# RWKV-7 recurrence in a hybrid block: state-free chunk products in one batch, and three VectorE instructions placed behind the product emitted last

## The chip, the cores and the metric

One NeuronCore of a Trainium2 chip runs the whole program in one launch. The metric is the device time in microseconds (us), lower is better.

## What is computed

A hybrid transformer block on 1024 tokens of width 1024: a forgetting attention and an RWKV-7 time mix side by side, then a gated convolutional feed-forward network. The change lies in the time mix, whose core is a recurrence over the tokens with a 64 x 64 state per head, 8 heads:

```python
def step(state, inp):
    r_t, w_t, k_t, v_t, a_t, b_t = inp
    sa = jnp.einsum('bhvk,bhk->bhv', state, a_t)
    state = state * w_t[:, :, None, :] + sa[..., None] * b_t[:, :, None, :] + v_t[..., None] * k_t[:, :, None, :]
    y_t = jnp.einsum('bhvk,bhk->bhv', state, r_t)
    return state, y_t
```

Here `w` is the decay, `a` the negated normalised key, `b` the normalised key times a learned rate. The result `y` is normalised per head, scaled, and gated. All values are float32.

## The kernel before

**Stages.** An opening stage normalises and modulates the input into `u`. Then come small low-rank products, then the recurrence, then the attention, the branch and output products, and the feed-forward network. Long products (128 x 512, float32r, each operand as a high and a low part, three products per pair) make up most of TensorE's work: the recurrence stage also holds the projections `ps_rkv`, `qk` and `gt` and the 256-wide `v`, all of them products with `u`, whose only task beside their own is to fill TensorE while a step of the recurrence waits.

**The recurrence.** Two heads and 512 tokens (half of the sequence, `hf`) make a unit; 4 head pairs `p` and 2 halves give 8 units, numbered `k` from 0. A unit is 8 chunks of 64 tokens. `pre` (L725) does what needs no state: it loads the log decays and rates (`cum`, `al`, L738 and L740), sums the decays by a scan on VectorE (L741) and exponentiates them on ScalarE, normalises the keys by `head_sums` (product `ssq`), multiplies keys by queries and rates chunk by chunk (product `p` into `E`, L786), and inverts the triangular 64 x 64 matrix of each chunk. The inversion takes 32 x 32 diagonal blocks: they go through DRAM scratch to a layout with one block per partition (`sm`, `M32`, L797 to L801), a substitution of 31 steps on VectorE, two instructions each (L809 writes `t`, L811 updates `E32`), and through DRAM again into `TT` (`se`, L814 and L822). Then follow transposes (`vt`, `at`, `tb`), the product `q` and the sums `bs`.

`main` (L855) joins the blocks: two VectorE transposes of `TT` into `X` (L866), the products `xi` and `zi`, then `uw`, then `mz`, which gives the two matrices `Zt` and `Mt` that take a state through a chunk. After that comes a loop over the 8 chunks. Each chunk has two kinds of small products into the PSUM tiles `sp` (next state) and `yp` (output): state-free ones (`sp<-UV,E`, `yp<-E,UV`, in `fixed`, L912) and ones with the state `S0` (`sp<-S,Mt`, `yp<-Zt,S`, L925 and L932). VectorE scales `sp` into the next state `S` (L929), which the next chunk's products need. `mu` and `va` close a unit by its normalisation.

**What sets the order.** TensorE runs in the order of emission. The class `Weave` (L48) emits: it keeps a nominal clock `now` in nanoseconds, adds a nominal cost for each product (`mm_cost`), and runs generators ("chains"). A chain emits a step and yields how long it wants to wait; until the next chain is due, `fill` emits long products. The main chain has rank 1 and the pre chain rank 2; a spawned chain has rank 0. VectorE, ScalarE, GpSimd and SyncE (which issues the transfers) get their order in this stage from the framework's scheduler: each instruction is placed by simulated times, after the ones that it depends on, and each engine then runs its own list strictly in that order.

The unit's `ready` (L802) is the nominal time before which `xi` is not emitted: 46000 ns (unit 0) or 38500 ns after the transfers into `M32`.

Of the kernel before, what the change touches and what calls it, by code (L numbers as in the profile page):

```python
# [9 lines left out]
F32 = mybir.dt.float32  # L10
# [37 lines left out]
class Weave:  # L48
# [67 lines left out]
    def run(self, chains):  # L116

        self.live = [[self.now, 1 + i, g] for i, g in enumerate(chains)]
        while self.live:
            due = min((c for c in self.live if c[0] <= self.now), key=lambda c: (c[1], c[0]), default=None)  # L120
            if due is None:
                self.fill(min(c[0] for c in self.live))
                continue
            wait = next(due[2], None)
            if wait is None:
                self.live.remove(due)
            else:
                due[0] = self.now + max(wait, 0.0)
# [3 lines left out]
def hybrid_block(ctx: ExitStack, tc: tile.TileContext, a, out):  # L132
# [4 lines left out]
    def mm(o, lhsT, rhs, start, stop, more=False):  # L137

        weave.mm_cost(o, lhsT, rhs)
        nc.tensor.matmul(o, lhsT, rhs, start=start, stop=stop, skip_group_check=more)  # L140
# [194 lines left out]
    with ExitStack() as es:  # L335
# [388 lines left out]

        def pre(k, p, hf):  # L725
# [15 lines left out]
            nc.vector.tensor_tensor_scan(cum, C("reset"), cum, initial=0.0, op0=ALU.mult, op1=ALU.add)  # L741
            el = chunk_tile("el", 1, NCU, CH + 1)
            nc.gpsimd.memset(el[:, :, 0:1], 1.0)
            nc.scalar.activation(el[:, :, 1:], c3(cum), AF.Exp, scale=-DEC)
            en = tmp("en")
            nc.scalar.activation(en, cum, AF.Exp, scale=DEC)
# [5 lines left out]
            yield from head_sums(ssq, ksq, parts[:, 0, :], parts[:, 1, :])  # L752
            rn = tmp("ksq")
# [48 lines left out]
            ready = weave.now + (46000 if k == 0 else 38500)  # L802
            E32 = chunk_tile("E32", 1, 8, 32)
            nc.gpsimd.tensor_copy(E32, C("einit").rearrange("p (j t) -> p j t", t=32))
            t32 = tmp("t32", 256)
            for s in range(31):
                J, W = s // 4 + 1, 31 - s
                tv = t32[:, 0 : J * W].rearrange("p (j w) -> p j w", w=W)
                tt(tv, E32[:, 0:J, s : s + 1].to_broadcast([128, J, W]),  # L809
                   M32[:, s : s + 1, s + 1 : 32].to_broadcast([128, J, W]), op=ALU.mult)  # L810
                tt(E32[:, 0:J, s + 1 : 32], E32[:, 0:J, s + 1 : 32], tv, op=ALU.add)  # L811
            se = scr.tile([2, NCU, 2, 32, 32], F32, tag="se", name=f"se{n}")
            for g in range(4):
                nc.sync.dma_start(  # L814
                    se.rearrange("h c b (j g) t -> (h c b) g j t", g=4)[:, g, :, :],
                    E32[g * 32 : g * 32 + 32, :, :])
            TT = chunk_tile("TT", 2, NCU, CH)
            for h in range(2):
                nc.gpsimd.memset(TT[h * 64 + 32 : h * 64 + 64, :, 0:32], 0.0)
                for b in range(2):  # L820
                    r0 = h * 64 + b * 32
                    nc.sync.dma_start(TT[r0 : r0 + 32, :, b * 32 : b * 32 + 32],  # L822
                                      se[h, :, b, :, :].rearrange("c s t -> s c t"))

# [30 lines left out]
        def main(k, p, hf):  # L855
# [8 lines left out]
            B1 = (slice(32, 64), slice(96, 128))  # L864
            for h in range(2):
                nc.vector.transpose(X[B0[h], :, :], TT[B0[h], :, 0:32])  # L866
            yield max(0, o["ready"] - weave.now)
# [44 lines left out]
            def fixed(c):  # L912

                alone = hf == 0 and c == 0
                for h in range(2):
                    mm(sp[HS[h], c, :], E[:, c, h, 2, :], UV[:, c, h, :], start=True, stop=alone)
# [1078 lines left out]
```

## Time and profile before

| what | us |
|---|---|
| median of 3 runs (lowest, highest) | 1701.3 (1697.85, 1704.96) |
| profiled execution, its own time | 1704.73 |
| its span in the trace | 1703.0 |
| TensorE busy, weight loads, VectorE, ScalarE, GpSimd | 1638.0, 1342.0, 1220.8, 808.6, 143.4 |
| recurrence stage in the trace | 151 to 655 |

How to read it: PE is TensorE, PEld its weight loads, DVE VectorE, ACT ScalarE, POOL GpSimd, SP the engine that issues most transfers. A row names the line, the engine, the operation, what it writes and reads (`sp<-UV,E`), the shape, the count, the busy time or the duration, and the idle time ahead of it with what ended it. Matmuls are pipelined and their ends are modelled, so the step from one start to the next tells the rate, not the duration. The small float32 products stand as two rows each, and those of the two heads start together.

### The profile page before, as it was taken

The numbers are of one execution on the slowest core, as the hardware profiler recorded it, in microseconds if no ns is written. First come the engines' busy times: TensorE is split into PE (matmuls) and PEld (weight loads), VectorE is DVE, ScalarE is ACT, GpSimd is POOL, SyncE is SP. The second block draws the span as 40 slices with busy tenths as digits, with TensorE's granted clock in tenths as the row PEclk, the third lists the DMA queues.
The fourth block names the chain that finished last, engine by engine and source line by source line (L and its number), as shares of the span: only waits on it lengthen the run. The fifth ranks groups of instructions, "written<-read, shape, count | busy, mean of one in ns | idle before, by whom it ended". The sixth has DMA issues, their size and how long they took to land.

```text
span 1703.0 us, 26042 instructions
## 1 busy us (share of the span) xinstructions
PE 1638.0 (96%) x9772; PEld 1342.0 (79%) x9772; DVE 1220.8 (72%) x2390; ACT 808.6 (47%) x1482; POOL 143.4 (8%) x175
## 2 busy tenths in 40 slices
PE   5899999998999998999999999999999999999998
PEld 4767777786877776988878888888888888888886
DVE  5776787778676633888877634897777777787677
ACT  5453334333444554766642323654444444454455
POOL 0010101110111003123112000000000000000000
PEclk8899999999999999999999999999999999999999
DMA  8487743533342326433277611132333233484463
GB/s 328 139 314 205 192 125 97 136 106 106 91 115 75 91 81 151 141 110 107 76 265 268 246 62 63 50 105 94 123 107 103 93 117 101 163 284 153 125 215 112
DMA packets 120974, 239.85 MB, mean 141 GB/s; under 512 B 39888, under 2 KB 48336, under 8 KB 120848
## 3 DMA queue, kind: packets, MB, share of 16 engines
q1 hardware_dynamic: 112896, 220.94, 40.0%
q0 software_dynamic: 7952, 17.25, 3.8%
q8 instruction: 77, 1.26, 0.3%
q14 instruction: 49, 0.40, 0.1%
HBM read 172.59 MB, written 65.54 MB: 140 GB/s over the span
## 4 chain that ended last, share of the span: by engine, by line
PE 79%; DVE 9%; DMA 6%; ACT 2%; issue 2%; SPq 1%; DVEq 0%; ACTq 0%
PE X L140 13%; PE D L140 12%; PE Y L140 6%; PE wo L140 5%; PE br L140 5%; PE gt L140 5%; PE rk_ps L140 4%; PE qk L140 4%; PE ps_rkv L140 4%; PE W L140 3%; PE lg L140 2%; PE v L140 2%; PE ov L140 2%; PE sp L140 2%; PE tp L144 2%
## 5 line engine op out<-in xcount | busy, mean ns | idle before, releaser
L140 PE MATMUL D<-op,op 128*128 128x512 f32 x924 | 209.8, 390 | 0.0
L140 PEld LDWEIGHTS D<-op,op 128*128 128x128 f32 x924 | 173.5, 188 | 36.2 <-DVE op L1258 0.3
L140 PE MATMUL X<-T_m,S 128*128 128x512 f32 x440 | 107.3, 390 | 0.2
L140 PEld LDWEIGHTS X<-T_m,S 128*128 128x128 f32 x440 | 82.5, 188 | 18.2 <-ACT x L1534 0.6
L1257 ACT CAST op<-g 128x512 fp32r<-128x512 f32 x77 | 47.8, 621 | 74.1 <-PE D L140 48.0
L1258 DVE TENSOR_TENSOR op<-g,op 128x512 fp32r<-128x512 f32 x77 | 53.0, 689 | 41.7 <-ACT op L1257 41.7
L1494 DVE SCALAR_TENSOR_TENSOR c<-ab,vec,c 128x512 f32<-128x512 f32 x88 | 65.9, 750 | 19.5 <-ACT c L1497 17.9
L809 DVE TENSOR_TENSOR t<-E,M 128x60 f32<-128x60 f32 (+24 forms) x248 | 57.9, 233 | 30.2 <-DMA M<-sm 24.9
L1458 DVE TENSOR_TENSOR S<-ur,S 128x512 fp32r<-128x512 f32 x66 | 45.5, 691 | 35.6 <-ACT S L1454 35.5
L263 DVE TENSOR_TENSOR lo_in<-raw_in,hi_in 128x512 fp32r<-128x512 f32 x84 | 56.5, 707 | 16.1 <-PE gt L140 13.9
L1454 ACT CAST S<-ur 128x512 fp32r<-128x512 f32 x66 | 41.0, 622 | 55.6 <-DVE ur L1447 30.6
L1458 DVE TENSOR_TENSOR A<-ur,A 128x512 fp32r<-128x512 f32 x64 | 44.1, 688 | 30.9 <-ACT A L1454 30.7
L261 ACT CAST hi_in<-raw_in 128x1024 fp32r<-128x1024 f32 x42 | 44.0, 1049 | 44.3 <-PE ps_rkv L140 16.0
L140 PE MATMUL Y<-T_h,A 128*128 128x512 f32 x264 | 63.5, 390 | 0.0
L140 PE MATMUL Y<-T_h,S 128*128 128x512 f32 x264 | 63.3, 390 | 0.0
L140 PE MATMUL X<-B_b,A 128*128 128x512 f32 x252 | 60.8, 391 | 0.0
L140 PE MATMUL W<-B_f,A 128*128 128x512 f32 x252 | 60.6, 390 | 0.0
L1079 ACT ACTIVATE P<-lg,nm 128x896 f32<-128x896 f32 (+3 forms) x64 | 47.4, 743 | 22.8 <-DVE nm L1075 22.6
L811 DVE TENSOR_TENSOR E<-E,t 128x60 f32<-128x60 f32 (+24 forms) x248 | 53.8, 217 | 5.8
L140 PEld LDWEIGHTS Y<-T_h,A 128*128 128x128 f32 x264 | 49.6, 188 | 10.3
L140 PEld LDWEIGHTS Y<-T_h,S 128*128 128x128 f32 x264 | 49.6, 188 | 10.3
L1454 ACT CAST A<-ur 128x512 fp32r<-128x512 f32 x64 | 39.9, 623 | 34.2 <-PE X L140 31.5
(473 smaller groups left out, 4169.0 us busy)
## 6 DMA issues: line engine op xcount, KB each, us to landing
raw_in<-in_w_in SPq DMA_DIRECT2D x50, 512.0 KB, 3.7
wm<-in_w_mod SPq DMA_DIRECT2D x48, 512.0 KB, 7.0
ur<-in_w_up SPq DMA_DIRECT2D x44, 512.0 KB, 4.2
g<-d_g SPq DMA_DIRECT2D x35, 512.0 KB, 4.0
d_g<-gs SPq DMA_DIRECT2D x44, 256.0 KB, 2.0
d_g<-c SPq DMA_DIRECT2D x33, 256.0 KB, 4.4
d_st<-qh SPq DMA_DIRECT2D x64, 128.0 KB, 2.5
d_gate<-gs SPq DMA_DIRECT2D x32, 256.0 KB, 2.9
```

The source lines that it names most:

```text
L140: nc.tensor.matmul(o, lhsT, rhs, start=start, stop=stop, skip_group_check=more)
L144: nc.tensor.transpose(o, i, eye)
L261: nc.scalar.copy(hi, raw)
L263: nc.vector.tensor_tensor(lo[:, c : c + NH], raw[:, c : c + NH], f32(hi[:, c : c + NH]), op=ALU.subtract)
L809: tt(tv, E32[:, 0:J, s : s + 1].to_broadcast([128, J, W]), M32[:, s : s + 1, s + 1 : 32].to_broadcast([128, J, W]), op=ALU.mult)
L811: tt(E32[:, 0:J, s + 1 : 32], E32[:, 0:J, s + 1 : 32], tv, op=ALU.add)
L1079: nc.scalar.activation(e[:, 0:n], lg[:, 0:n], AF.Exp, bias=nm[:, 0:1], accum_out=nm[:, 1:2])
L1257: nc.scalar.copy(hi, src)
L1258: tt(lo, src, f32(hi), op=ALU.subtract)
L1454: nc.scalar.copy(hi, src)
L1458: tt(lo, src, f32(hi), op=ALU.subtract)
L1494: stt(c, ab[:, x + hf * NH : x + hf * NH + NH], V("conv_w", 22 * x + i), c, op0=ALU.mult, op1=ALU.add)
```

## The change

Four edits, all in the recurrence:

- **State-free products in one go.** `fixed` is gone. All 8 chunks' state-free products stand directly behind `mz`; the loop over the chunks holds only the products with the state. Only the first chunk's products open the accumulation of the two PSUM banks.
- **VectorE instructions behind the product emitted last.** A helper `behind` adds an ordering without a semaphore between a VectorE instruction and the last emitted matmul, so that the scheduler does not place it earlier. It is used for the scan of the decays (now also emitted after `ssq` instead of ahead of it), the first instruction of the substitution, and the two transposes into `X` (now emitted 1500 nominal ns ahead of `xi`, before at the head of `main`).
- **The inversion as a chain of its own**, `inverse`, spawned 8500 nominal ns after the transfers into `M32`; `ready` of unit 0 goes from 46000 to 47500.
- **`beside`.** A due step of the pre chain is held back, with fill, if a step of the main chain or of a spawned chain comes within 2600 nominal ns, and follows that step without fill between.

```diff
-    def run(self, chains):
+    def run(self, chains, beside=0.0):
...
+        led = False
         while self.live:
             due = min((c for c in self.live if c[0] <= self.now), key=lambda c: (c[1], c[0]), default=None)
-            if due is None:
-                self.fill(min(c[0] for c in self.live))
+            lead = min((c[0] for c in self.live if c[1] < 2), default=None)
+            if due is None or (due[1] > 1 and not led and lead is not None and lead < self.now + beside):
+                self.fill(min(c[0] for c in self.live) if due is None else lead)
+                led = False
                 continue
+            led = beside > 0 and (led or due[1] < 2)
...
-        nc.tensor.matmul(o, lhsT, rhs, start=start, stop=stop, skip_group_check=more)
+        weave.last = nc.tensor.matmul(o, lhsT, rhs, start=start, stop=stop, skip_group_check=more)
+
+    def behind(i):
+        tc.add_manual_dep(i.ins, weave.last.ins.name, NOSYNC)
...
+        def inverse(n, M32, TT, chunk_tile, tmp):
...
+                i = tt(tv, E32[:, 0:J, s : s + 1].to_broadcast([128, J, W]),
+                   M32[:, s : s + 1, s + 1 : 32].to_broadcast([128, J, W]), op=ALU.mult)
+                if s == 0:
+                    behind(i)
+                tt(E32[:, 0:J, s + 1 : 32], E32[:, 0:J, s + 1 : 32], tv, op=ALU.add)
...
-            nc.vector.tensor_tensor_scan(cum, C("reset"), cum, initial=0.0, op0=ALU.mult, op1=ALU.add)
-            el = chunk_tile("el", 1, NCU, CH + 1)
...
             yield from head_sums(ssq, ksq, parts[:, 0, :], parts[:, 1, :])
+            behind(nc.vector.tensor_tensor_scan(cum, C("reset"), cum, initial=0.0, op0=ALU.mult, op1=ALU.add))
+            el = chunk_tile("el", 1, NCU, CH + 1)
...
-            ready = weave.now + (46000 if k == 0 else 38500)
+            ready = weave.now + (47500 if k == 0 else 38500)
             TT = chunk_tile("TT", 2, NCU, CH)
+            weave.spawn(inverse(n, M32, TT, chunk_tile, tmp), 8500)
...
+            yield max(0, o["ready"] - weave.now - 1500)
             for h in range(2):
-                nc.vector.transpose(X[B0[h], :, :], TT[B0[h], :, 0:32])
-            yield max(0, o["ready"] - weave.now)
+                behind(nc.vector.transpose(X[B0[h], :, :], TT[B0[h], :, 0:32]))
+            yield 1500
...
-            def fixed(c):
-
+            for c in range(NCU):
                 alone = hf == 0 and c == 0
                 for h in range(2):
-                    mm(sp[HS[h], c, :], E[:, c, h, 2, :], UV[:, c, h, :], start=True, stop=alone)
+                    mm(sp[HS[h], c, :], E[:, c, h, 2, :], UV[:, c, h, :], start=c == 0, stop=alone, more=True)
                 for h in range(2):
-                    mm(yp[HS[h], c, :], UV[:, c, h, :], E[:, c, h, 1, :], start=True, stop=alone)
-
-            fixed(0)
+                    mm(yp[HS[h], c, :], UV[:, c, h, :], E[:, c, h, 1, :], start=c == 0, stop=alone, more=True)
...
-                    fixed(c + 1)
...
-        weave.run([main_chain(), pre_chain()])
+        weave.run([main_chain(), pre_chain()], beside=2600.0)
```

Lines below the first edits move down (the product helper from L140 to L144, the transposes into `X` from L866 to L881). The counts of products, transfers and VectorE instructions stay the same, and so do TensorE's order ahead of unit 0's `xi` and all order behind the last unit. Stretches of long products between small ones in the recurrence go from 133 to 123.

**TensorE, unit 1 behind `mz`.** Before, each chunk's state-free products (`sp<-UV,E`, `yp<-E,UV`) stand between long products (`qk`) and that chunk's products with the state (`S`):

```order
L140 MATMUL mz_14_2840<-E_1_1785,Wt_1_2764 64x128 x8
L140 MATMUL sp_1_2852<-UV_1_1787,E_1_1785 64x64 x2
L140 MATMUL yp_1_2851<-E_1_1785,UV_1_1787 64x64 x2
L140 MATMUL qk_0_2824<-u_hi,hi_in_2480 128x512 x6
L140 MATMUL qk_0_2824<-u_lo,hi_in_2480 128x512 x6
L140 MATMUL sp_1_2852<-S_07_2419,Mt_1_2828 64x64 x2
L140 MATMUL yp_1_2851<-Zt_1_2827,S_07_2419 64x64 x2
L140 MATMUL qk_0_2824<-u_lo,hi_in_2480 128x512 x2
L140 MATMUL qk_0_2824<-u_hi,lo_in_2481 128x512 x4
L140 MATMUL sp_1_2852<-UV_1_1787,E_1_1785 64x64 x2
L140 MATMUL yp_1_2851<-E_1_1785,UV_1_1787 64x64 x2
L140 MATMUL sp_1_2852<-S_10_2884,Mt_1_2828 64x64 x2
```

Now, at the same place (the first two small rows stand eight times in a row):

```order
L144 MATMUL mz_14_2843<-E_1_1783,Wt_1_2788 64x128 x8
L144 MATMUL sp_1_2855<-UV_1_1785,E_1_1783 64x64 x2
L144 MATMUL yp_1_2854<-E_1_1783,UV_1_1785 64x64 x2
...
L144 MATMUL ssq_1_2813<-kp_1_2761,blk_r 128x512 x2
L144 MATMUL qk_0_2782<-u_hi,lo_in_2464 128x512 x5
L144 MATMUL qk_1_2930<-u_hi,hi_in_2463 128x512 x5
L144 MATMUL sp_1_2855<-S_07_2427,Mt_1_2831 64x64 x2
L144 MATMUL yp_1_2854<-Zt_1_2830,S_07_2427 64x64 x2
L144 MATMUL qk_1_2930<-u_hi,hi_in_2463 128x512 x3
L144 MATMUL qk_1_2930<-u_lo,hi_in_2463 128x512 x3
L144 MATMUL sp_1_2855<-S_10_2938,Mt_1_2831 64x64 x2
L144 MATMUL yp_1_2854<-Zt_1_2830,S_10_2938 64x64 x2
```

The state-free products have left the loop; six long products still separate one state step from the next, and the pre chain's `ssq` now follows small products directly.

**VectorE, the transposes into `X` of unit 4.** Before, they stand in the middle of unit 3's state steps (`S`) and of the next keys (`kr`, `ar`, `bk`):

```order
L762 SCALAR_TENSOR_TENSOR ar_1_4250<-kr_1_4247,nkk,el_1_4162 128x512
L352 MEMSET sh_rkv_4451 128x1
L929 TENSOR_SCALAR S_11_4305<-sp_1_4237,pcd_1_2866 128x64
L763 SCALAR_TENSOR_TENSOR kr_1_4247<-kr_1_4247,vec,al_1_4159 128x512
L866 STREAM_TRANSPOSE X_0_4698<-TT_0_3868 32x256
L764 TENSOR_TENSOR bk_1_4249<-kr_1_4247,en_1_4165 128x8x64
L767 TENSOR_SCALAR al_1_4159<-al_1_4159,vec,oka 128x512
...
L929 TENSOR_SCALAR S_12_4321<-sp_1_4237,pcd_1_2866 128x64
```

Now they stand behind unit 3's last state step, behind the masks of the products `p` (L823) and the copies of the transposes `at` (L850):

```order
L941 TENSOR_SCALAR S_16_4410<-sp_1_4231,pcd_1_2911 128x64
...
L959 SCALAR_TENSOR_TENSOR y_1_4424<-mu_1_4426,y_1_4424 128x512
L823 TENSOR_TENSOR E_1_4427<-p_2_104_4491,cst_120 128x4x128
L823 TENSOR_TENSOR E_1_4427<-p_2_114_4492,cst_120 128x4x128
L992 TENSOR_TENSOR vs_0_4505<-v_0_4463,vs_0_4505 128x4x64
L850 COPY QA_1_4428<-at_1_4546 64x4x64 x4
L881 STREAM_TRANSPOSE X_0_4601<-TT_0_3837 32x256 x2
L992 TENSOR_TENSOR vs_1_4568<-v_1_4509,vs_1_4568 128x4x64
L968 SCALAR_TENSOR_TENSOR y_1_4424<-y_1_4424,vec,rs_1_4591 128x512
```

The first transpose stood two rows behind the state step `S_11` of unit 3, and the second three rows on; now both stand together, behind five more state steps.

**VectorE, the scan of unit 5.** Before, it stands early in unit 4's substitution (`t`, `E`), ahead of weight parts (`lo_in`) and of an evacuation (`k<-ps_rkv`):

```order
L852 TENSOR_TENSOR bon_0_4049<-bs_0_3960,v_2739 128x512
L811 TENSOR_TENSOR E_0_3798<-E_0_3798,t_0_3800 128x2x25
L809 TENSOR_TENSOR t_0_3800<-E_0_3798,M_0_3793 128x48
L741 SCALAR_TENSOR_TENSOR cum_1_4157<-cst_120,cum_1_4157 128x512
L811 TENSOR_TENSOR E_0_3798<-E_0_3798,t_0_3800 128x2x24
L263 TENSOR_TENSOR lo_in_4078<-raw_in_4075,hi_in_4077 128x512 x2
L809 TENSOR_TENSOR t_0_3800<-E_0_3798,M_0_3793 128x69
L358 SCALAR_TENSOR_TENSOR k_3355<-ps_rkv_4020,omu,sh_rkv_4071 128x512
```

Now it stands near the end of that substitution, behind the evacuations of `mz` (L919, L920):

```order
L919 TENSOR_TENSOR Zt_1_4206<-mz_14_4219,ar_1_2902 128x256
L920 TENSOR_TENSOR Mt_1_4207<-mz_14_4219,cst_120 128x256
...
L740 TENSOR_TENSOR t_0_3967<-E_0_3965,M_0_3832 128x28
L781 SCALAR_TENSOR_TENSOR cum_1_4157<-cst_120,cum_1_4157 128x512
L744 TENSOR_TENSOR E_0_3965<-E_0_3965,t_0_3967 128x7x4
...
L800 TENSOR_TENSOR ar_1_4278<-r_3376,el_1_4267 128x512
```

The scan moved from the 8th to the 28th of the substitution's 31 steps, and the `ar` that needs its exponentials (`el`) follows four rows behind it.

More of the change, by code (lines that the diff above doesn't have):

```diff
@@ L924, in main @@
                     for h in range(2):
-                        mm(sp[HS[h], c, :], Mt[HS[h], c, :], S0[HS[h], :], start=False, stop=True)
+                        mm(sp[HS[h], c, :], Mt[HS[h], c, :], S0[HS[h], :], start=False, stop=True, more=True)
                 S1 = None
@@ L931, in main @@
                     for h in range(2):
[L932 removed]
+                        mm(yp[HS[h], c, :], S0[HS[h], :], Zt[HS[h], c, :], start=False, stop=True, more=True)
                 if c + 1 < NCU:
                     yield 1150
[L935 removed]
                 S0 = state[p] = S1
```

48 lines of the change are left out of this document (23 added, 25 removed).

## The prediction

> **What bounds the kernel now.** I read the page first, then the waits of TensorE (PE) and VectorE (DVE) in the recurrence stage, then the busy time by stretches, and last the timeline at single places. The page:
>
> ```profile
> PE 1638.0 (96%) x9772; PEld 1342.0 (79%) x9772; DVE 1220.8 (72%) x2390; ACT 808.6 (47%) x1482; POOL 143.4 (8%) x175
> ```
>
> PE is the bound, and all work behind the last unit keeps its order, so the change can win only what PE loses in the stage from 151 to 655 us. Busy time there and in three short stretches (length; PE, PEld, DVE, ACT, POOL; granted clock, DMA share, GB/s):
>
> ```profile
> 151.00:655.00 504.00, 486.29 (x4349) 387.77 (x4348) 338.16 (x964) 214.19 (x374) 57.17 (x78) 0.99 0.41 113
> 228.00:238.00 10.00, 7.02 (x78) 5.16 (x78) 6.74 (x22) 2.96 (x7) 0.72 (x3) 0.83 0.48 133
> 417.00:430.00 13.00, 9.54 (x72) 6.82 (x70) 7.46 (x18) 2.86 (x4) 1.97 (x4) 0.87 0.27 75
> 528.00:538.00 10.00, 7.65 (x57) 5.20 (x56) 5.91 (x13) 3.11 (x5) 0.40 (x1) 0.83 0.27 72
> ```
>
> PE stands still for 504.0 - 486.3 = 17.7 us, and around three of the waits its granted clock drops. Who PE waited for in the stage (total, times, longest), and below it DVE's waits for transfers:
>
> ```profile
> PE sp L140 <- DVE S L929: 8.6, 5, 3.5
> PE xi L140 <- DVE X L866: 3.0, 2, 1.6
> PE p L140 <- DVE bk L769: 2.0, 1, 2.0
> PE ps_rkv L140 <- DVE k L358: 1.6, 1, 1.6
> PE at L144 <- DVE E L789: 1.0, 1, 1.0
> PE qk L140 <- DVE ql L384: 0.9, 1, 0.9
> ```
>
> ```profile
> DVE t L809 <- DMA M<-sm: 24.9, 7, 6.7
> DVE X L866 <- DMA TT<-se: 23.3, 12, 4.9
> DVE cum L741 <- DMA cum<-d_lora: 10.8, 5, 5.5
> ```
>
> Every wait of PE is for DVE, and DVE itself stood 59 us (24.9 + 23.3 + 10.8) at the head of its list waiting for transfers. These are the three instructions that the change moves.
>
> **The state-free products.** One chunk's turn before (start, length), its weight loads, and two groups of the stage (count, busy, mean ns, idle ahead): the state-free products and `q`, the nearest batch of like shape.
>
> ```profile
> 255.02 0.34 PE L140 MATMUL sp<-UV,E 128*64 128x64 f32 x4
> 255.19 0.29 PE L140 MATMUL yp<-E,UV 128*64 128x64 f32 x4
> 255.40 0.33 PE L140 MATMUL sp<-S,Mt 64*64 64x64 f32 x4
> 255.57 0.28 PE L140 MATMUL yp<-Zt,S 64*64 64x64 f32 x4
> 255.78 0.73 PE L140 MATMUL ps_rkv<-u_hi,hi_in 128*128 128x512 f32 x2
> 257.37 0.34 PE L140 MATMUL sp<-UV,E 128*64 128x64 f32 x4
> ```
>
> ```profile
> 255.02 0.20 PEld L140 LDWEIGHTS sp<-UV,E 128*64 128x64 f32 x4 [0.44 <-DVE S L929]
> ...
> 255.13 0.20 PEld L140 LDWEIGHTS yp<-E,UV 128*64 128x64 f32 x4
> ```
>
> ```profile
> L140 PE MATMUL sp<-UV,E 128*64 128x64 f32 x256 | 21.6, 248 | 8.6 <-DVE S L929 8.6
> ...
> L140 PE MATMUL q<-UV,E 64*64 64x64 f32 x256 | 10.0, 222 | 0.1
> ```
>
> From the first state-free product to the first one with the state pass 255.40 - 255.02 = 0.38 us. In a batch the next chunk's loads follow at the pace of these loads, 0.11 us for each four rows, so a chunk takes 0.22 to 0.23 us and nothing is paid for going over to the 64-row form. At `q`'s rate a chunk's 8 of 256 rows take 8 x 10.0 / 256 = 0.31 us. The saving is 0.07 to 0.16 us a chunk; I take 0.15, since the loads are of the very same products. The first chunk of each of the 8 units stands behind `mz` as before, so 7 x 8 = 56 chunks count: 56 x 0.15 = **8.4 us** (3.9 to 9.0). What covered the state's round trip through DVE stays: the first state-free product of a chunk waited for `S` as well (the row has all 8.6 us of those waits), behind the same six long products.
>
> The Trainium skill, page "TensorE: Matmul & The Clock Gate", section "Part 3: Packing small matmuls — row/col tiling", speaks against the batch: a weight load overlaps running products only when it goes to other rows of the array, and these products use all 128. By that rule this term would be about zero. The trace disagrees: loads of 0.20 us and products of 0.34 and 0.29 us for two such groups fit into 0.38 us, so they overlap already.
>
> **Fewer changes between long and small products.** A long product's own pace, from the largest group of the page:
>
> ```profile
> L140 PE MATMUL D<-op,op 128*128 128x512 f32 x924 | 209.8, 390 | 0.0
> ```
>
> 209.8 / 924 = 0.227 us. The six between 255.78 and 257.37 took 1.59 us where 6 x 0.227 = 1.36, so going in and out costs 0.23. The new order has 10 stretches of long products fewer (133 to 123). Small products that meet directly still pay something, as the step from the state-free to the state form does (0.38 - 0.23 = 0.15 at most). I take 0.14 each, **1.4 us** (0.8 to 2.3).
>
> **DVE's waits for transfers.** How one of them reaches PE, on DVE and then on PE:
>
> ```profile
> 417.18 0.74 DVE L763 SCALAR_TENSOR_TENSOR kr<-kr,vec,al 128x512 f32<-128x512 f32 x1
> 421.72 0.43 DVE L866 STREAM_TRANSPOSE X<-TT 32x256 f32<-32x256 f32 x1 [3.80 <-DMA TT<-se]
> ...
> 423.68 0.28 DVE L929 TENSOR_SCALAR S<-sp,pcd 128x64 f32<-128x64 f32 x1
> ```
>
> ```profile
> 424.02 0.47 PE L140 MATMUL sp<-UV,E 128*64 128x64 f32 x4 [3.46 <-DVE S L929]
> ...
> 425.25 2.44 PE L140 MATMUL ps_rkv<-u_hi,lo_in 128*128 128x512 f32 x5
> 427.53 0.40 PE L140 MATMUL ps_rkv<-u_hi,hi_in 128*128 128x512 f32 x1
> ```
>
> The same instructions at three more places, with DVE's wait in brackets:
>
> ```profile
> 393.11 1.23 DVE L741 TENSOR_TENSOR_SCAN cum<-cst,cum 128x512 f32<-128x512 f32 x1 [2.98 <-DMA cum<-d_lora]
> ```
>
> ```profile
> 488.37 0.43 DVE L866 STREAM_TRANSPOSE X<-TT 32x256 f32<-32x256 f32 x1 [4.16 <-DMA TT<-se]
> ```
>
> ```profile
> 531.54 0.43 DVE L866 STREAM_TRANSPOSE X<-TT 32x256 f32<-32x256 f32 x1 [3.17 <-DMA TT<-se]
> ```
>
> At 421.72 a transpose whose `X` no product needs before this chunk loop is over holds the state step behind it, and PE stands 3.46 us. Of the five waits for `S` one more is of this kind, behind 531.54: 2.35 us in the stretch 528 to 538 (10.00 - 7.65). The scan at 393.11 does the same to `k` (1.6), the transpose at 488.37 to `E` (1.0), and unit 0's transposes are late themselves (3.0). Together 3.46 + 2.35 + 1.6 + 1.0 + 3.0 = **11.4 us**. Behind the change the transposes stand behind the state steps and the scan follows its transfer by about 4.7 nominal us, so the first four waits go; of unit 0's, where PE comes eight long products (8 x 0.227 = 1.8 us) later, I leave 1.0. That is 10.4 us. What was hidden under these waits is short: DVE's own arrears at the other three `S` waits (8.6 - 5.8 = 2.8 us), which I leave as they are, as I do `p` and `qk`.
>
> **The clock.** From 424.02 to 427.53 pass 3.51 us, where a chunk's turn (255.78 - 255.02 = 0.76) and five long products (5 x 0.227) take 1.90: 1.6 us lost to the lower clock. The three stretches above with 0.83 to 0.87 lie behind three waits that go; 3 x 1.6 = **4.8 us** (0 to 4.8). The Trainium skill, page "TensorE: Matmul & The Clock Gate", section "What's actually happening", puts the throttle behind an idle window of about 3.4 us; by that only the 3.46 us wait would count and the term would be 1.6. The rows show it behind 2.35 us too, so the measurement decides.
>
> **What the change adds.** The substitution starts 8500 nominal ns behind the transfers into `M32`, and the transposes come only 1.5 us ahead of `xi`. For unit 5, whose margin is among the smallest:
>
> ```profile
> L801 SPq DMA_DIRECT2D M<-sm x4: 364/416/425, 444.5 to 445.8; - x4
> ```
>
> ```profile
> 448.90 1.16 DVE L809 TENSOR_TENSOR t<-E,M 128x31 f32<-128x31 f32 x1 [3.00 <-DMA M<-sm]
> ```
>
> ```profile
> L140 PE MATMUL xi<-X,E x32: 190/191/213, 497.2 to 497.7; 32*32 32x32 f32 x32
> L866 DVE STREAM_TRANSPOSE X<-TT x2: 433/434/436, 488.4 to 489.4; 32x256 f32<-32x256 f32 x2
> ```
>
> `X` is done at 489.8 and `xi` starts at 497.2, a margin of 7.4 us. The first substitution step moves from 448.9 to 444.5 + 8.5 = 453.0, 4.1 us later; the unit's chunk loop, shorter by 7 x 0.15, and the 1.0 us wait before it take some 2 more. About 1 us is left, less if DVE, which carries the same 338 us in a shorter stage, is slower with the chain, more since the 3.0 us that it lost at 448.9 now do other work. Some units will wait; the scan, moved behind `ssq`, also delays `p`:
>
> ```profile
> L741 DVE TENSOR_TENSOR_SCAN cum<-cst,cum x8: 1211/1224/1226, 155.8 to 507.3; 128x512 f32<-128x512 f32 x8
> L744 ACT ACTIVATE el<-cum x8: 630/632/634, 157.1 to 508.6; 128x512 f32<-128x512 f32 x8
> ```
>
> 1.22 and 0.63 us go onto that way. From unit 2 on `p` waits for the last state step of the unit two before (L777) anyway; in units 0 and 1 PE's wait at `p` can grow by these 1.9 us. SP's transfers behind a late `se` carry weights that are needed 48 products (11 us) later. I book **4 us** of new waits (0 to 12).
>
> **Sum.** 8.4 + 1.4 + 10.4 + 4.8 - 4.0 = 21 us. The profiled execution took 1704.7 us (span 1703.0), so 1683.7 by its own time; it lies 3.4 us above the median of 1701.3, so I forecast **1681 us**, with 1671 (9.0 + 2.3 + 11.4 + 4.8 and the arrears of 2.8 = 30.3, no new waits) to 1687 (the batch at 7, a third of the clock term gone, 8 us of new waits: 7 + 1.4 + 10.4 + 3.2 - 8 = 14.0) as this case's own range.
>
> **Rivals.** (1) *The waits come back elsewhere.* DVE works as much in a stage that is 4% shorter, and three of five waits for `S` already had no transfer ahead of them. If all 11.4 us of waits and their clock return at other places, the products alone win 8.4 + 1.4 = 9.8: about 1691 (1685 to 1697). That the three orderings name the wrong instructions falls under it; the rows of the waits speak against it. (2) *`xi` waits in every unit.* The substitution of unit 5 takes from 448.9 to the transposes at 488.4 with transfers, 40 us. If, denser with the state steps, it stretches by a fifth, 8 us, `X` comes 7 us late, 1 us of margin taken off, and each such wait brings 1.6 us of low clock. In 7 units that is 7 x (7 + 1.6) = 60, less 25 us won: slower by 35, 1736. The point from which it decides is a mean lateness of 25 / 7 = 3.6 us at `xi`; against it speaks that DVE loses no time at `M32` any more. (3) *The batch does not overlap its loads*, the rule above: without that term 1689.
>
> **Chances.** Forecast 0.70, rival 1 0.20, rival 2 0.04, rival 3 0.04, other 0.02. The range, 1671 to 1693, takes in the forecast's own range, rival 3 and the better half of rival 1. Half a percent, 8.5 us, is about what a measurement of this kernel can tell from no change: faster by more than that is below 1692.8, which holds the forecast, rival 3 and half of rival 1, 0.70 + 0.04 + 0.10 = 0.84; slower is rival 2, 0.04; 0.12 lies within.
>
> **What would show it.** In the profile after: the state-free products of a unit as one group of some 1.9 us behind `mz`; a chunk's turn of about 2.0 us instead of 2.35 (255.02 to 257.37); no wait of DVE for `TT` or `cum` ahead of an `S`; the three stretches of low clock gone; the stage some 21 us shorter. The forecast is wrong if waits for `X` at `xi` add up to more than some 12 us, or if PE's waits for `S` stay near 8.6 us.

## The result and the profile after

The changed kernel takes 1675.3 us (median of 4 runs, 1675.23 to 1676.12); the kernel before, run beside it, 1699.57 (1696.57 to 1704.96). The ratio is 0.985, with a 95% interval of 0.9832 to 0.9867. Forecast were 1681 us, in a range of 1671 to 1693, and that it would be faster by over half a percent.

In the changed kernel the lines have other numbers: a matmul is L144, a substitution step L740 and L744, the scan L781, the transposes L881, the state step L941. PE's line of the page, and then the busy time of the recurrence stage (columns as before). The stage is cut at the same two products as the 504.00 us before; it starts 0.75 us earlier.

```profile
PE 1622.3 (97%) x9772; PEld 1333.2 (80%) x9772; DVE 1227.8 (73%) x2390; ACT 808.3 (48%) x1482; POOL 147.8 (9%) x175
```

```profile
150.25:625.30 475.05, 469.80 (x4349) 379.25 (x4348) 346.05 (x965) 214.90 (x375) 61.19 (x78) 1.00 0.44 121
```

The stage is 28.95 us shorter. PE's idle time in it went from 17.7 to 475.05 - 469.80 = 5.25 us, so 12.45 us are waits; the other 16.5 us are busy time, of which 5.1 are the clock (see the point on it below). The profiled execution took 1675.3 us where that of before took 1704.7, near its slowest run; so the traces differ by 29.4 us and the medians by 24.3.

What PE waited for in the stage, and DVE's waits for transfers (total, times, longest):

```profile
PE qk L144 <- DVE v L365: 2.2, 1, 2.2
PE sp L144 <- DVE S L941: 1.5, 3, 0.9
PE zi L144 <- ACT X L888: 0.6, 1, 0.6
PE q L144 <- DVE QA L850: 0.4, 1, 0.4
```

```profile
DVE X L881 <- DMA TT<-se: 8.2, 3, 4.1
DVE t L740 <- DMA M<-sm: 5.7, 2, 5.4
DVE cum L781 <- DMA cum<-d_lora: 5.0, 1, 5.0
```

The waits for `S` fell from 8.6 to 1.5 us; those at `xi`, `k`, `p` and `E` are gone; of the new ones the largest has 2.2 us. DVE stands for transfers 18.9 us instead of 59.

The batch of unit 0, its first and last groups, and behind it one turn of the chunk loop:

```profile
244.19 0.34 PE L144 MATMUL sp<-UV,E 128*64 128x64 f32 x4
244.35 0.29 PE L144 MATMUL yp<-E,UV 128*64 128x64 f32 x4
244.47 0.29 PE L144 MATMUL sp<-UV,E 128*64 128x64 f32 x4
...
245.87 0.29 PE L144 MATMUL sp<-UV,E 128*64 128x64 f32 x4
245.99 0.29 PE L144 MATMUL yp<-E,UV 128*64 128x64 f32 x4
```

```profile
255.47 0.33 PE L144 MATMUL sp<-S,Mt 64*64 64x64 f32 x4
...
257.44 0.33 PE L144 MATMUL sp<-S,Mt 64*64 64x64 f32 x4
```

A group of four rows follows the last at 0.12 us, so a chunk takes 0.23 to 0.24 us. The turn is 257.44 - 255.47 = 1.97 us where it was 2.35, with the same six long products in it. The two groups of state-free products over the whole stage (21.6 and 18.5 us busy before):

```profile
L144 PE MATMUL sp<-UV,E 128*64 128x64 f32 x256 | 15.7, 225 | 0.0
...
L144 PE MATMUL yp<-E,UV 128*64 128x64 f32 x256 | 15.4, 222 | 0.0
```

### The profile page after: what moved, and what is told of

The parts are those of the page before. It is cut to its first block, busy times and chain, and to the rows that moved or that the text cites. A ratio compares the mean times of both kernels' runs of the same rounds, so it can differ in the third digit from the quotient of the medians.

```text
span 1673.2 us, 26056 instructions
## 1 busy us (share of the span) xinstructions
PE 1622.3 (97%) x9772; PEld 1333.2 (80%) x9772; DVE 1227.8 (73%) x2390; ACT 808.3 (48%) x1482; POOL 147.8 (9%) x175
## 4 chain that ended last, share of the span: by engine, by line
PE 82%; DVE 9%; DMA 4%; ACT 3%; issue 2%; SPq 1%; POOL 0%; DVEq 0%; ACTq 0%
PE X L144 13%; PE D L144 13%; PE Y L144 6%; PE gt L144 6%; PE ps_rkv L144 6%; PE wo L144 5%; PE br L144 5%; PE rk_ps L144 4%; PE W L144 3%; PE v L144 2%; PE lg L144 2%; PE ov L144 2%; PE tp L151 2%; PE qk L144 2%; PE low L144 1%
## 5 line engine op out<-in xcount | busy, mean ns | idle before, releaser
L144 PE MATMUL D<-op,op 128*128 128x512 f32 x924 | 209.8, 389 | 0.0
L144 PEld LDWEIGHTS D<-op,op 128*128 128x128 f32 x924 | 173.3, 188 | 36.3 <-DVE op L1269 0.3
L144 PE MATMUL X<-T_m,S 128*128 128x512 f32 x440 | 107.2, 390 | 0.1
L144 PEld LDWEIGHTS X<-T_m,S 128*128 128x128 f32 x440 | 82.4, 188 | 18.2 <-ACT T_m L1694 0.5
L740 DVE TENSOR_TENSOR t<-E,M 128x60 f32<-128x60 f32 (+24 forms) x248 | 56.0, 226 | 12.0 <-DMA M<-sm 5.7
L144 PE MATMUL Y<-T_h,A 128*128 128x512 f32 x264 | 63.5, 389 | 0.0
L144 PE MATMUL Y<-T_h,S 128*128 128x512 f32 x264 | 63.3, 389 | 0.0
L744 DVE TENSOR_TENSOR E<-E,t 128x60 f32<-128x60 f32 (+24 forms) x248 | 56.8, 229 | 5.8
L144 PE MATMUL X<-B_b,A 128*128 128x512 f32 x252 | 60.8, 390 | 0.0
L144 PE MATMUL W<-B_f,A 128*128 128x512 f32 x252 | 60.6, 389 | 0.0
L144 PEld LDWEIGHTS Y<-T_h,A 128*128 128x128 f32 x264 | 49.5, 188 | 10.4
L144 PEld LDWEIGHTS Y<-T_h,S 128*128 128x128 f32 x264 | 49.5, 188 | 10.3
L1465 ACT CAST A<-ur 128x512 fp32r<-128x512 f32 x64 | 39.8, 623 | 34.1 <-PE X L144 29.4
```

The costliest lines, as they stand in the source:

```text
L144: weave.last = nc.tensor.matmul(o, lhsT, rhs, start=start, stop=stop, skip_group_check=more)
L740: i = tt(tv, E32[:, 0:J, s : s + 1].to_broadcast([128, J, W]), M32[:, s : s + 1, s + 1 : 32].to_broadcast([128, J, W]), op=ALU.mult)
L1465: nc.scalar.copy(hi, src)
```

## The experiments

**Theory and rivals.** By the prediction, some 8.4 us come from the steps between the two forms of small products, and the rest from DVE no longer standing at the head of its list for transfers, with the clock that drops behind PE's waits. The rivals: the gain beside the batch comes from PE's new order and not from VectorE's; or one of the three orderings carries it alone. All twelve runs in one table, then what each was for. PE's order is word for word the changed kernel's in those marked =, so that only the place of DVE's instructions (and of the transfers behind them) differs; in *spread*, all of PE's order but the place of the state-free products.

| kernel | median us | ratio to before (95%) | median less the changed kernel's, us |
|---|---|---|---|
| batch alone | 1694.58 | 0.9960 (0.9946 to 0.9974) | 19.3 |
| spread: state-free products by chunk | 1682.37 | 0.9893 (0.9879 to 0.9908) | 7.1 |
| all but the batch | 1696.21 | 0.9966 (0.9951 to 0.9982) | 20.9 |
| = all three orderings undone | 1690.62 | 0.9935 (0.9914 to 0.9957) | 15.3 |
| = transposes undone | 1677.46 | 0.9854 (0.9828 to 0.9880) | 2.2 |
| = scan undone | 1675.93 | 0.9861 (0.9840 to 0.9881) | 0.6 |
| = substitution undone | 1682.93 | 0.9896 (0.9879 to 0.9914) | 7.6 |
| = scan and transposes undone | 1684.22 | 0.9905 (0.9891 to 0.9919) | 8.9 |
| without `beside` | 1688.23 | 0.9927 (0.9909 to 0.9945) | 12.9 |
| `ready` of unit 0 later by 3000 | 1699.39 | 0.9995 (0.9984 to 1.0007) | 24.1 |
| = unit 0's transposes right ahead of `xi` | 1674.53 | 0.9842 (0.9825 to 0.9859) | -0.8 |
| = substitution later | 1740.89 | 1.0239 (1.0225 to 1.0254) | 65.6 |

The last column compares runs that were not made beside each other: the kernel before took 1699.57 us beside the changed kernel and 1700.44 to 1700.78 beside these. With single runs several us apart as well, a difference of 2 us or less tells nothing.

**The batch alone.** The kernel before, with this:

```diff
-            fixed(0)
+            for c in range(NCU):
+                alone = hf == 0 and c == 0
+                for h in range(2):
+                    mm(sp[HS[h], c, :], E[:, c, h, 2, :], UV[:, c, h, :], start=c == 0, stop=alone, more=True)
+                for h in range(2):
+                    mm(yp[HS[h], c, :], UV[:, c, h, :], E[:, c, h, 1, :], start=c == 0, stop=alone, more=True)
             yield 2400
             for c in range(NCU):
...
-                    fixed(c + 1)
```

> The kernel before with the state-free products of a unit in one go behind mz; the scan, the substitution, the transposes and the order of the two chains stay as before. Theory of the prediction: the batch is worth 56 x 0.15 = 8.4 us of PE time (the step from the state-free to the state form falls away), and the waits for transfers stay; about 1691 us where before has 1699.6 (1687 to 1694). Rival, the loads don't overlap: no gain, 1699. Rival, the batch is a gain only beside the new order because PE now waits for S where the state-free products had covered the round trip: 1696 or more, with PE's waits for S above 15 us.

Measured: 1694.58 where the kernel before took 1700.64 beside it, 6 us (4.4 to 9.2 by the interval). PE's waits for `S` were 7.4 us (8.6 before), so the state's round trip stayed covered; its idle time in the stage was 19.7 us, 2 more than before, which is about what is missing to 8.4. The rival without overlap is out.

**All but the batch, and the batch spread.** First, the changed kernel with `fixed` as before:

```diff
-            for c in range(NCU):
+            def fixed(c):
...
+            fixed(0)
             yield 2400
...
                     yield 1150
+                    fixed(c + 1)
```

> The changed kernel with the state-free products again chunk by chunk, all else as changed. Theory: the 8.4 us come back, 1675.3 + 8.4 = about 1684 (1681 to 1686), with no new wait of PE. If batch and order help each other: above 1688; if the batch is worth nothing here: 1675.

It lost 20.9 us: by its number the rival that batch and order help each other. The stage holds other work, though. From a product ahead of it to the first one of the attention part, in this kernel and in the changed one:

```profile
144.67:647.21 502.54, 495.44 (x4422) 397.33 (x4420) 350.60 (x976) 221.65 (x388) 66.57 (x90) 1.00 0.44 123
```

```profile
146.32:627.13 480.81, 475.56 (x4373) 383.81 (x4372) 350.80 (x972) 216.92 (x379) 64.34 (x84) 1.00 0.44 123
```

There are 4422 instructions of PE in it and not 4373: the planner's clock counts the state-free products where they are emitted, so it dealt 48 long products (10.9 us at 0.227) out ahead of the attention part, where they are missed later. The attention part has 10.9 us less work and takes 1.1 us longer (258.6 against 257.6 us), so 12.0 us are lost behind the stage; in it PE stands 17.1 us where it stood 12.6. The comparison does not price the batch. Hence a second kernel, whose planner believes in the batch (against the first):

```diff
+            t0 = weave.now
             fixed(0)
+            weave.now = t0 + NCU * (weave.now - t0)
             yield 2400
...
+                    t0 = weave.now
                     fixed(c + 1)
+                    weave.now = t0
```

> The changed kernel with the state-free products of chunk c + 1 again behind chunk c, but with the planner's clock set as if they stood in one go, so that PE's list is word for word the changed kernel's in everything else (all but the batch had let the long products be dealt out differently, 48 more of them ahead of the attention part). Theory: only the 8.5 us of steps between the two forms come back, 1675.3 + 8.5 = about 1684 (1681 to 1686). Rival, what batch alone showed (6 us) is all that it is worth: 1681. Rival, the 21 us that all but the batch lost belong to the batch itself: above 1690.

Measured: 1682.37, 7.1 us lost. Its stage between the same two products, where PE stands as little as in the changed kernel (4.7 us idle against 5.25):

```profile
144.89:633.73 488.84, 484.16 (x4373) 388.24 (x4372) 352.28 (x972) 217.13 (x379) 63.90 (x84) 1.00 0.43 121
```

PE's busy time is 484.16 - 475.56 = 8.6 us more: the 8.4 us of the prediction, by PE alone.

**All three orderings undone.** The changed kernel with the three edits that stand below with the single kernels made together; the batch and `beside` are kept.

> The changed kernel with all three orderings undone (scan, substitution and transposes where they were before), the batch kept, PE's own order the same word for word. Theory: the waits of 11.4 us and the clock of 4.8 us come back, about 1675.3 + 16.2 = 1691 (1686 to 1694), with runs several us apart as those of before were (1696.6 to 1705.0). Rival, the gain beside the batch comes from PE's new order and not from VectorE: 1675 to 1678, runs within 1 us.

Measured: 1690.62, 15.3 us lost, with PE's order unchanged; so the rival that PE's order makes the gain is out. The stage, and the three largest of PE's waits:

```profile
144.74:642.19 497.45, 480.16 (x4374) 385.94 (x4372) 347.04 (x972) 216.78 (x379) 63.25 (x84) 0.99 0.43 119
```

```profile
PE sp L144 <- DVE S L941: 5.8, 8, 1.4
PE qk L144 <- DVE v L365: 3.3, 1, 3.3
PE q L144 <- ACT UV L908: 2.3, 1, 2.3
```

Idle time is 497.45 - 480.16 = 17.3 us, 12.1 more than in the changed kernel, and busy time 4.6 us more. The sum of the prediction holds, 11.4 of waits and 4.8 of clock, but the waits are not those that it named: the rest is spread over eight further places of 1.1 us or less. Of the busy time 3.4 us are the clock: it is 0.50 for 3.41 us from 229.60 and again from 553.86, behind the waits of 3.3 and 2.3 us. With the 8.6 us of the batch these 15.3 us make 23.9 of the 24.3 us that the whole change won.

**Each ordering by itself.** Transposes back at the head of `main`:

```diff
+            for h in range(2):
+                nc.vector.transpose(X[B0[h], :, :], TT[B0[h], :, 0:32])
             yield max(0, o["ready"] - weave.now - 1500)
-            for h in range(2):
-                behind(nc.vector.transpose(X[B0[h], :, :], TT[B0[h], :, 0:32]))
             yield 1500
```

> The changed kernel with the two transposes of a unit back at the head of main, not ordered behind a product; PE's own order is the same, word for word. Theory: DVE again stands at transposes ahead of state steps, PE waits for S, and the clock drops behind it: 3.46 + 2.35 + 1.0 us of waits and two to three stretches at 1.6 us, so 1675.3 + 6.8 + 3.2 = about 1685 (1680 to 1688), and the spread of its runs grows. Rival, the order of the transposes is without weight once the substitution is started late: 1675 to 1677.

Measured: 1677.46, not told apart from the changed kernel. DVE stands at the transposes as long as it did before the change, and PE hardly feels it:

```profile
DVE X L880 <- DMA TT<-se: 24.9, 10, 5.2
```

```profile
PE sp L144 <- DVE S L941: 1.9, 4, 0.9
```

This is the largest part of the prediction's largest term (3.46 + 2.35 + 1.0 us of waits), and by itself it is not there. It does not follow that a late transpose cannot hold PE. In this kernel only two of the ten waits stand close ahead of a state step: 1.55 us at 261.31, whose state PE needs only in the next unit, and 1.51 us at 408.95, behind which PE waits 0.9 us. Behind the others the next state step comes some 20 us later or more. The scan, `el` and `en` back ahead of `ksq`:

```diff
+            nc.vector.tensor_tensor_scan(cum, C("reset"), cum, initial=0.0, op0=ALU.mult, op1=ALU.add)
...
             ksq = tmp("ksq")
...
             yield from head_sums(ssq, ksq, parts[:, 0, :], parts[:, 1, :])
-            behind(nc.vector.tensor_tensor_scan(cum, C("reset"), cum, initial=0.0, op0=ALU.mult, op1=ALU.add))
```

> The changed kernel with the scan and the two exponentials back ahead of the squares, the scan not ordered behind a product; PE's order the same word for word. Theory: DVE stands at the scan for cum again, in five units some 2 us, of which one reached PE before (1.6 us at k): about 1677 (1675 to 1680). Rival, the scan alone made the waits of S as well: above 1682. Rival, moving the scan back helps because el and en come earlier for bk: 1674.

Measured: 1675.93, not told apart either, with runs from 1674.25 to 1680.59; in its trace PE waits 2.4 us at `p`. The substitution at once behind the transfers into `M32` (an empty chain keeps the planner's times):

```diff
-                if s == 0:
-                    behind(i)
...
-            weave.spawn(inverse(n, M32, TT, chunk_tile, tmp), 8500)
+            for _ in inverse(n, M32, TT, chunk_tile, tmp):
+                pass
+            weave.spawn(iter(()), 8500)
```

> The changed kernel with the substitution started at once behind the transfers into M32, as before, not 8500 nominal ns later and not ordered behind a product; PE's order the same word for word. Theory: DVE's waits for M32 come back (24.9 us before, none of which PE was seen to wait for directly), and X is ready up to 4 us earlier; 1675 to 1680, most likely 1677. Rival, this is the ordering that carries the gain (25 us of DVE's lost time): above 1682.

Measured: 1682.93, 7.6 us lost: the rival, this ordering carries half of the 15.3. How a wait at `M32` reaches PE, on DVE and then on PE, in this kernel:

```profile
486.13 0.19 DVE L740 TENSOR_TENSOR t<-E,M 128x31 f32<-128x31 f32 x1 [3.59 <-DMA M<-sm]
...
488.37 0.75 DVE L365 SCALAR_TENSOR_TENSOR k<-ps_rkv,omu,sh_rkv 128x512 f32<-128x512 f32 x1
...
489.80 0.68 DVE L862 COPY QA<-q 128x512 f32<-128x512 f32 x1
...
491.86 0.41 DVE L906 COPY Wt<-uw 128x256 f32<-128x256 f32 x1
```

```profile
492.42 0.33 PE L144 MATMUL mz<-E,Wt 64*64 64x128 f32 x2 [1.63 <-DVE E L742]
```

DVE loses 3.59 us at 486.13 and then works without a gap through what has queued up (`k`, `QA` and `Wt` among it); 6 us later `mz` is 1.63 us late for `Wt`. The row of PE's wait names a substitution step (L742) and no transfer. So a wait for a transfer also costs as arrears, and the waits for `S` without a transfer right ahead of them, which the prediction left as they were, are mostly of this kind: 4.8 us at seven places here, 1.5 at three in the changed kernel. Ahead of four of the seven (298.58, 460.51, 462.84 and 508.20, 3.3 us together) DVE's list has no gap over 0.08 us back to a wait at `M32` (276.52, 432.68 and 486.13). Ahead of the three that had no transfer near in the kernel before (301.94, 355.43 and 415.80) it has none back to such a wait or to one at the scan (292.90, 333.01 and 393.11).

Then the substitution late as in the changed kernel, and the first two of these three edits together:

> The changed kernel with the scan and the transposes where they were before and only the substitution started late behind a product; PE's list the same word for word. If each ordering has its own price: 1675.3 + 2.2 + 0.6 = about 1678 (1676 to 1680). Rival, the 4.9 us by which all three undone (15.3) cost more than the three one by one (2.2 + 0.6 + 7.6 = 10.4) belong to scan and transposes together: about 1683.

Measured: 1684.22, 8.9 us lost where the two alone lost 2.2 and 0.6. The rival is right: undone together the two cost what neither costs alone, and the excess of all three over the single ones lies here. Idle time in the stage is 10.5 us (5.3 more), busy time 5.4 us more. One of the waits is the one that the prediction read in the kernel before, in unit 4, on DVE and then on PE:

```profile
415.65 0.43 DVE L880 STREAM_TRANSPOSE X<-TT 32x256 f32<-32x256 f32 x1 [2.94 <-DMA TT<-se]
416.02 0.23 DVE L941 TENSOR_SCALAR S<-sp,pcd 128x64 f32<-128x64 f32 x1
```

```profile
416.31 0.33 PE L144 MATMUL sp<-S,Mt 64*64 64x64 f32 x4 [1.72 <-DVE S L941]
```

So a transpose that waits ahead of a state step does hold PE, when it stands there. The largest wait, for `v` in unit 0, and the clock of the six us behind it:

```profile
230.50 0.80 PE L144 MATMUL qk<-u_hi,hi_in 128*128 128x512 f32 x1 [3.31 <-DVE v L365]
```

```profile
230.50:236.50 6.00, 6.00 (x43) 4.52 (x44) 5.39 (x23) 3.68 (x7) 0.19 (x1) 0.50 0.54 146
```

The same two in the changed kernel:

```profile
228.11 0.50 PE L144 MATMUL qk<-u_hi,hi_in 128*128 128x512 f32 x1 [2.23 <-DVE v L365]
```

```profile
228.10:232.10 4.00, 3.99 (x46) 3.11 (x47) 3.31 (x14) 0.00 (x0) 0.00 (x0) 1.00 0.84 308
```

There the clock is whole. Here it is 0.50 for 6.82 us (from 229.79), and again for 3.41 us behind the wait of 1.72 us (from 417.53): 5.1 of the 5.4 us of busy time. That the wait of 2.23 us left the clock whole is not owed to its length alone (last section).

**Without `beside`:**

```diff
-        weave.run([main_chain(), pre_chain()], beside=2600.0)
+        weave.run([main_chain(), pre_chain()], beside=0.0)
```

> The changed kernel without the rule that lets a step of the preparing chain go beside one of the main chain (beside=0). Theory: some ten more stretches of long products at 0.14 us each, 1677 (1675.5 to 1678). Rival, that rule also placed the preparing steps where DVE is free: above 1680.

Measured: 1688.23, 12.9 us lost, and again 48 long products are dealt out ahead of the attention part:

```profile
144.57:642.69 498.12, 490.27 (x4421) 394.32 (x4420) 350.92 (x976) 222.99 (x388) 61.16 (x84) 1.00 0.44 122
```

Of 17.3 us in the stage, 48 x 0.227 = 10.9 are that work, 2.6 are idle time and 3.8 busy time (1.7 of it one stretch of 3.41 us at half clock). The attention part, without them, should be 10.9 us shorter and is only 4.4 us shorter (253.2 against 257.6 us, from the first attention product to the 3500th product from the end). So in these traces 6.4 us are lost in the stage and 6.5 behind it. The stage's part is above the 1.4 us at which the prediction took this edit.

**Unit 0, where the 2.2 us wait is left.** First with a later `ready`:

```diff
-            ready = weave.now + (47500 if k == 0 else 38500)
+            ready = weave.now + (50500 if k == 0 else 38500)
```

> The changed kernel with the time set for xi in the first unit 3000 nominal ns later (50500). In the changed kernel's trace the transposes of that unit still stand 3.8 us for their transfer and PE then waits 2.2 us for v. Theory: that wait goes and nothing is late behind it: 1673 (1672.5 to 1674). Rival, the whole chain of units comes 3 us later and another wait takes its place: 1675 to 1677.

Measured: 1699.39. All of the gain is gone: PE's order is dealt out anew, PE waits 11.3 us at `xi` in five places, and the 48 products are ahead of the attention part here too. This did not test what it was meant for. So, with PE's order held, only for unit 0:

```diff
             yield max(0, o["ready"] - weave.now - 1500)
+            if k == 0:
+                yield 1500
             for h in range(2):
                 behind(nc.vector.transpose(X[B0[h], :, :], TT[B0[h], :, 0:32]))
-            yield 1500
+            if k:
+                yield 1500
```

> The changed kernel with the first unit's transposes emitted right ahead of xi instead of 1.5 nominal us ahead of it; PE's list the same word for word. Theory: v is no longer behind the transposes on DVE, PE's wait of 2.2 us for it goes, and xi, which came 1.9 us behind X, is hardly later: about 1673 (1672.5 to 1674). Rival, X is then the late one and PE waits for it as long: 1675 to 1676.

Measured: 1674.53 (1670.3 to 1675.8), not told apart from the changed kernel. The wait for `v` is gone and PE waits 2.4 us at `xi` instead: by the rows the rival.

**The substitution later.** This is the prediction's rival 2, tried by force:

```diff
-            weave.spawn(inverse(n, M32, TT, chunk_tile, tmp), 8500)
+            weave.spawn(iter(()), 8500)
+            weave.live.append([weave.now + 14500, 3, inverse(n, M32, TT, chunk_tile, tmp)])
```

> The changed kernel with the substitution started 14500 instead of 8500 nominal ns behind the transfers into M32; PE's list the same word for word. By the changed kernel's trace X would be late at xi by about 4.1 us in the first unit, 1.1 in the fourth and 5.8 in the last, 11 us together, and DVE would stand at transposes some us longer in two more: with the clock behind long waits 1686 to 1692. That is the mechanism of the prediction's rival 2, which there decided from a mean lateness of 3.6 us. If the chain has more room than the trace shows: below 1679.

Measured: 1740.89, 65.6 us lost. The delay was longer than planned. The added chain has the lowest rank and went behind all other steps, in unit 2 to 296.2 us where the transfers had been issued by 277.4; in the changed kernel these are 279.3 and 275.3. The rows: PE's largest wait of the stage, and unit 2's `xi`:

```profile
PE xi L144 <- DVE X L882: 48.2, 12, 12.1
```

```profile
340.50 0.28 PE L144 MATMUL xi<-X,E 32*32 32x32 f32 x2 [12.11 <-DVE X L882]
```

It does not show at what delay the loss begins, but that little on the way behind `X` hides it: in unit 2 the first step stands 18.8 us behind the last transfer's issue instead of 4.0, 14.8 more, and 12 of them arrive at `xi`, and the granted clock of the whole run fell to 0.966 from 0.986.

## Why the prediction was right, point by point

- **State-free products, 8.4 us.** Right: 8.6 us of PE's busy time by the kernel that spreads them, 6 and 7 us by the medians of the two clean kernels. What covered the state's round trip did stay. The Trainium skill, page "TensorE: Matmul & The Clock Gate", section "Part 3: Packing small matmuls — row/col tiling", has a load overlap running products only on other rows of the array; the batch, on all 128 rows, goes at 0.12 us a group with loads of 0.2 us, so the measurement decides against the rule here.
- **Changes between long and small products, 1.4 us.** Right in size, though no run has it by itself: of the 16.5 us of busy time 8.6 are the batch and 4.6 came back when the orderings were undone. Of the 3.3 us left, 1.7 are a stretch of half clock that did not come back there, so some 1.6 us are left for this term. By the kernel without `beside` the rule is worth 6.4 us in the stage with the waits that the old dealing-out brings. The number of stretches is not ten fewer in the traces: between the first `ssq` and the last `va` they have 127 before, 120 in the changed kernel, and 141 without `beside`. The term was counted as a number of stretches alone; that the rule also decides what stands beside what, and how much is left for the attention part, was missed.
- **DVE's waits, 10.4 us.** The sum was right (12.1 us of idle time came back with all three orderings undone), the working was not. "At 421.72 a transpose whose `X` no product needs before this chunk loop is over holds the state step behind it" reads the row rightly, and the kernel with scan and transposes undone shows it again, with 1.72 us of PE. What failed is to price each edit by the places at which the old order had its wait: with the transposes alone undone DVE stands 24.9 us, but mostly elsewhere, and at `S` PE loses 0.9 us by it. And the 2.8 us of arrears, "which I leave as they are", could not be left apart: they were what DVE's waits at `M32` and the scan had left over. The substitution, for whose waits at `M32` the prediction booked nothing, carries 7.6 us. That the sum came out all the same is in part luck.
- **The clock, 4.8 us.** Right: the kernel before has three stretches of 3.41 us at half clock in the stage, 5.1 us together, and the changed kernel none; with the orderings undone two came back, 3.4 of the 4.6 us of busy time. The three before:

```profile
232.94:236.35 3.41, 3.41 (x19) 2.67 (x13) 2.76 (x11) 1.36 (x3) 0.19 (x1) 0.50 0.55 169
424.08:427.49 3.41, 3.41 (x21) 2.76 (x22) 2.03 (x4) 0.36 (x1) 0.00 (x0) 0.50 0.07 24
533.31:536.72 3.41, 3.41 (x17) 2.25 (x16) 3.29 (x6) 1.25 (x2) 0.00 (x0) 0.50 0.16 60
```

- **New waits, -4 us.** They did not come. In the traces the stage won 12.45 us of idle time where 10.4 - 4.0 = 6.4 were booked; these 6 us, the new waits and the arrears, are most of what the forecast lacks. The unit with the least margin at `xi` is the last one, on DVE and then on PE:

```profile
576.71 0.90 DVE L881 STREAM_TRANSPOSE X<-TT 32x256 f32<-32x256 f32 x2 [4.12 <-DMA TT<-se]
```

```profile
577.85 0.69 PE L144 MATMUL xi<-X,E 32*32 32x32 f32 x32
```

  `X` is done at 577.6, 0.2 us ahead. In unit 5, which the prediction worked out, the first step came 5.4 us behind the issue of `M32`'s transfers and not 8.5 (428.1 to 433.5); ahead of the transfers that feed them SP had stood 3.1 us for the masks (L823), so they were issued late. The delay of `p` by the moved scan went the other way: 0 to 0.8 us in the nine kernels that have the scan late, 1.1 to 2.4 in the five with it early.
- **The 2.2 us at `qk`** take the place of `xi`'s 3.0 in unit 0: the transposes there still stand 3.8 us for `TT` and hold `v`. The prediction left 1.0 us.
- **Rivals.** The waits did not come back elsewhere. Rival 2's mechanism is real; the kernel keeps 0.2 to 7 us of margin in each unit.

Open stays which edit makes the order that deals 48 products more or less: three kernels met it by small changes of the planner's times, and lost 6.5 to 12 us behind the stage.

## What to carry over

Price the place of an instruction that waits for a transfer with the order of the critical engine held fixed, and undo orderings together as well as one by one: here two that cost 2.2 us or less alone cost 8.9 us together. An engine that is not the bound pays for its waits later, as arrears, so the releaser in the row of a wait need not be its cause. Where a planner deals out filler, compare how much of it each kernel puts ahead of the next stage before reading a price from the difference.

## What was not expected of the hardware

Whether the clock drops behind a wait of PE is not decided by the wait's length alone. In the kernel with the substitution undone it stays whole behind a wait of 1.92 us (up to 226.38) and falls behind one of 1.67 us (up to 508.20). The traces record the granted clock in stretches, and in all fourteen of them these begin and end on a grid with a step of 3.41 us, which lies differently against the kernel's start in each trace. The steps around the two waits:

```profile
222.57:225.98 3.41, 1.89 (x9) 1.24 (x7) 1.27 (x3) 0.60 (x1) 0.49 (x2) 1.00 0.59 141
225.98:229.39 3.41, 3.01 (x41) 2.31 (x42) 2.60 (x14) 0.00 (x0) 0.00 (x0) 1.00 0.90 309
505.88:509.29 3.41, 1.74 (x14) 1.13 (x13) 3.27 (x13) 0.00 (x0) 0.00 (x0) 1.00 0.22 41
509.29:512.70 3.41, 3.41 (x16) 2.25 (x15) 1.18 (x7) 0.00 (x0) 0.00 (x0) 0.50 0.36 135
```

The longer wait is cut by the grid at 225.98, and neither step has PE idle for more than 1.52 us; the shorter lies whole in one step, PE is idle for 1.67 of its 3.41 us, and the next step has half the clock. So it is in all fourteen traces between 150 and 600 us: each of the 25 drops begins at the end of a step in which PE stood for 0.46 of it or more, and of the 1780 steps with the clock whole behind them none has PE idle for more than 0.50. The changed kernel's wait of 2.23 us is cut into 1.17 and 1.06 us (at 227.05) and leaves the clock whole; the wait of 2.19 us at the same place with the transposes undone has 1.70 us in one step, and the clock falls for 3.41 us. So a difference of some 2 us between two traces can be luck of where the grid lies. The Trainium skill, page "TensorE: Matmul & The Clock Gate", section "What's actually happening", puts the drop behind an idle window of about 3.4 us; the step of the grid agrees with that figure, but a window that is half idle was enough here.
